# Where TensorE's operands begin in SBUF: one place mod 256 for high and low moving weights, and the row order of two-row pieces

## The chip, the cores and the metric

One NeuronCore of a Trainium2 chip runs the whole program in one launch. The metric is the device time in microseconds (us), the median of several executions. A profile of one execution stands beside it; its span runs from the first to the last instruction of the program.

## The reference: what is computed

Two transformer blocks on one sequence of 256 tokens of width 1024, all in float32. The first block normalises `x`, projects it with `w_in` into differential attention (8 heads), retention (4 heads) and two gates, mixes both branches, and adds a feed-forward layer (1024 to 4096 and back) and a gated embedding. The second block has an mLSTM mixer and a gated feed-forward layer with a causal convolution of width 3:

```python
def conv_ffn(x, w_up, conv_w, conv_b, w_down):
    u = causal_dwconv(x @ w_up, conv_w, conv_b)
    gate = u[..., :D_FF_2]
    val = u[..., D_FF_2:]
    return (jax.nn.silu(gate) * val) @ w_down      # 2816 rows in, 1024 columns out
```

A last RMS norm gives the output, 256 x 1024.

## The kernel before, in words

**Products in three passes.** Each operand of a large product is split into a high part (the value rounded to the matmul's `float32r` format, by ScalarE, line 198) and a low part (the rest, by VectorE, line 208). A product is then high x high + low x high + high x low, three matmuls (called passes, `q` = 0, 1, 2) that add up in PSUM. The low x low term is left out.

**Slabs.** All weights come in slabs of 1024 rows by 256 columns, in a fixed order (`_plan`). A slab has two halves of four 128-row pieces, and each half is one load of 512 KB, one high tile `hi_<slab>_<half>` and one low tile `lo_<slab>_<half>`. Loads go through a ring of four `raw` buffers on the SyncE queue; high and low tiles have rings of six. The down projection's slabs `dn0` to `dn10` are 256 rows by 1024 columns instead.

**Steps.** Three kinds of steps use the slabs, and they differ in which operand is stationary (loaded into the array by LDWEIGHTS) and which is moving (streamed through it):
- `b` steps (`pe_b`, line 257): the weights are stationary, activations move. Most slabs: `q`, `k`, `ga`, `gb`, `wd`, `wr`, `wo`, `f1`, `f2` (both named `f` in profiles), `pg`, `mq`, `mk`, `mw`, `ug`, `uv`, and likewise `wp` (lines 967 to 969).
- `a` steps (`pe_a`, line 267, and `step_wide`, line 340, for `mv0` alone): the activations are stationary and the weights move. Slabs `va0` to `va3`, `vr0` to `vr3`, `gr0` to `gr3`, `mv0` to `mv3`, `mo0` to `mo3`.
- the down projection (`pe_down`, line 1389): activations `gh`, `gl` (high and low) are stationary, the weights `dn` move. 528 matmuls, with the pass that comes first rotating from one output piece to the next.

Every such matmul is 128x128 by 128x256. A slab of an `a` or `b` step has 48: two halves, two column (or token) halves, four rows, three passes. Within a half `_steps` sets the order: it cuts the rows into pieces and goes through each piece pass by pass. At hooks between steps stand transposes and small products of the attention, the retention and the mLSTM, many of them in plain float32 with two passes of the engine.

**Places.** A tile of the high or low ring is 1088 columns of four bytes, 17 x 256 bytes, and a big activation tile 2112 columns, 33 x 256 bytes. In the built program both rings begin at multiples of 256 bytes. So an operand begins at a multiple of 256 bytes plus its *place*: `slot_of` shifts a weight tile by 16 columns (64 bytes) per unit of place, and `_place` gives the unit for high and low by the slab's name. Activations have no shift, so they are at 0.

**Joint steps.** Seven pairs of slabs (`JOINT`, among them `pg0`+`pg1`, `mw0`+`mw1`, `ug0`+`uv0`) are taken together: rows 0 to 3 of both, then rows 4 and 5 of both, then 6 and 7 of both (`joint`). These last are the two-row pieces. A norm's product with two passes (`pv_n`) stands among them in `pg` and `ug`.

What else counts below: `tu_m` are the transposes of the mLSTM's output `hn`, which VectorE writes at line 801; `w_m` and `ws_m` are the mLSTM's decay weights.

Of the kernel before, what the change touches and what calls it, by code (L numbers as in the profile page):

```python
# [10 lines left out]
F32 = mybir.dt.float32  # L11
F32R = mybir.dt.float32r
# [4 lines left out]
P = 128  # L17
# [88 lines left out]
def _place(name):  # L106

    n = name[0:2]
    if n in ("gr", "mv") or name in ("dn4", "dn5", "dn6"):
        return 3, 3  # L110
    if n in ("va", "vr", "mo", "dn"):
        return 1, 3
    if n == "wp":
        return 0, 2
    return 3, 1


def _steps(ks, m):

    ks = list(ks)  # L120
    cuts = {(4, 0): (1, 3), (4, 1): (2, 2), (2, 0): (2,), (2, 1): (1, 1), (3, 0): (1, 2), (3, 1): (3,)}[len(ks), m]
    steps = []
    for n in cuts:
        steps += [(q, k) for q in range(3) for k in ks[:n]]
        ks = ks[n:]
    return steps
# [3 lines left out]
def block_kernel(ctx: ExitStack, tc: tile.TileContext, I, out):  # L130
# [5 lines left out]
    big = ctx.enter_context(tc.tile_pool(name="big", bufs=11))  # L136
    work = ctx.enter_context(tc.tile_pool(name="work", bufs=2))
    psum = ctx.enter_context(tc.tile_pool(name="psum", bufs=4, space=bass.MemoryType.PSUM))

    def bigt(name, dt=F32, cols=2048):  # L140
        return big.tile([P, 2112], dt, tag="big", name=name)[:, 0:cols]

    def c8(t):
        return t.rearrange("p (c t) -> p c t", t=T)
# [13 lines left out]
    def pr(ap):  # L158
        return ap.rearrange("p (c t) -> p c t", c=2)
# [23 lines left out]
    def slot_of(tag, i, s):  # L183

        name = slabs[i][0]
        kk, cw = len(_rows(slabs[i])[s]), _width(slabs[i])
        pitch = -(-cw // 64) * 64
        sh = 16 * _place(name)[tag == "lo"]
        t = wpool.tile([P, 1088], F32R, tag=tag, name=f"{tag}_{name}_{s}", bufs=NBUF)
        return t[:, sh:sh + kk * pitch].rearrange("p (k n) -> p k n", k=kk)[:, :, 0:cw]  # L190
# [58 lines left out]
    def pe_b(ps, i, xh, xl, ks, m, start, stop):  # L249

        kk = geometry(i)[0]
        o = ps[:, m * T:(m + 1) * T]
        sl = slice(m * P, (m + 1) * P)
        steps = _steps(ks, m)
        for n, (q, k) in enumerate(steps):
            wv = (lo_t if q == 2 else hi_t)[i, k // kk]
            TE.matmul(o, lhsT=wv[:, k % kk, sl], rhs=(xl if q == 1 else xh)[:, k, :], start=start and n == 0,  # L257
                      stop=stop and n == len(steps) - 1, skip_group_check=True)

    def pe_a(ps, i, xh, xl, ks, t, start, stop):  # L260

        o = ps[:, t * T:(t + 1) * T]
        ts = slice(t * P, (t + 1) * P)
        steps = _steps(ks, t)
        for n, (q, k) in enumerate(steps):
            wv = (lo_t if q == 2 else hi_t)[i, k // 4]
            TE.matmul(o, lhsT=(xl if q == 1 else xh)[:, k, ts], rhs=wv[:, k % 4, :], start=start and n == 0,  # L267
                      stop=stop and n == len(steps) - 1, skip_group_check=True)
# [60 lines left out]
    def step_wide(name, xh, xl):  # L329

        i = index[name]
        cw = _width(slabs[i])
        pss = [mmbank(f"ps_{name}_0"), aux(f"ps_{name}_1")]

        def piece(s):
            for t in range(2):
                ts = slice(t * P, (t + 1) * P)
                ks = _rows(slabs[i])[s]
                for q, k in _steps(ks, t):
                    TE.matmul(pss[t][:, 0:cw], lhsT=(xl if q == 1 else xh)[:, k, ts],  # L340
                              rhs=(lo_t if q == 2 else hi_t)[i, s][:, k - ks[0], :], start=k == 0 and q == 0,
                              stop=k == 7 and q == 2, skip_group_check=True)

        halves(i, piece)
        after(i)
        return pss
# [42 lines left out]
    with tc.manual_schedule():  # L389
        S.preload_act_table_set(LNEXP)  # L390

        x = bigt("x0")
        xT = c8(x)
        par = const.tile([P, NPAR + PAD], F32, name="par")[:, 0:NPAR]
# [18 lines left out]
        nc.gpsimd.dma_start(out=ident, in_=I["c_ident"])  # L413
        lamt = wk("lamt", 768, tag="lg")[:, 0:T].rearrange("p (j d) -> p j d", j=4)
        cD = bigt("cD")
        maskT = const.tile([P, 384], F32, name="maskT")

# [10 lines left out]
        def rs_act(v, w, name, parts=P):  # L428
# [3 lines left out]
            return y0  # L432

        hh, hl = bigt("hh", F32R), bigt("hl", F32R)
        hhv, hlv = c8(hh), c8(hl)
        goff = _offsets()
# [32 lines left out]
        def split_plain(src, hv, lv):  # L469
            S.activation(hv, src, ACTF.Copy)  # L470
            yield
            V.tensor_tensor(out=lv, in0=src, in1=hv.bitcast(F32), op=ALU.subtract)
# [127 lines left out]
        va = bigt("va").rearrange("p (t n) -> p t n", t=2)  # L600
# [191 lines left out]
        gr, ga = bigt("gr").rearrange("p (t n) -> p t n", t=2), c8(bigt("ga"))  # L792
# [494 lines left out]
        gh, gl = {}, {}  # L1287
# [18 lines left out]
        def conv(ps, c0, s, name):  # L1306
            y = pr(ring[:, s % 4, :])
            u = pr(ps)
            if s < 2 * NRAWUP:
                u = pr(wk(f"u_{name}", 512, tag="qt"))  # L1310
                V.tensor_tensor(out=u, in0=pr(ps), in1=b2(r6), op=ALU.mult)
                yield
            for c in range(2):
                cc = c0 + c
                S.activation(y[:, c, :], u[:, c, :], ACTF.Identity, scale=cvt[:, 88 + cc:89 + cc], bias=cvt[:, 132 + cc:133 + cc])
            yield
            for c in range(2):
                cc = c0 + c
                V.scalar_tensor_tensor(out=y[:, c, 1:T], in0=u[:, c, 0:T - 1], scalar=cvt[:, 44 + cc:45 + cc], in1=y[:, c, 1:T],
                                       op0=ALU.mult, op1=ALU.add)  # L1320
                V.scalar_tensor_tensor(out=y[:, c, 2:T], in0=u[:, c, 0:T - 2], scalar=cvt[:, cc:cc + 1], in1=y[:, c, 2:T],
                                       op0=ALU.mult, op1=ALU.add)
            yield
# [10 lines left out]
        def post_uv(j):  # L1334
            def f(ps):
                yield from conv(ps, 22 + 2 * j, 2 * j + 1, f"v{j}")
                y = pr(ring[:, (2 * j + 1) % 4, :])
                V.tensor_tensor(out=y, in0=ug.pop(j), in1=y, op=ALU.mult)
                yield
                b, r = divmod(2 * j, 8)  # L1340
                if r == 0:
                    gh[b], gl[b] = c8(bigt(f"gh{b}", F32R)), c8(bigt(f"gl{b}", F32R))
                yield from split_plain(y, gh[b][:, r:r + 2, :], gl[b][:, r:r + 2, :])
            return f

# [30 lines left out]
        cuts = {0: ((0, 512), (512, 1024)), 1: ((0, 512), (512, 768), (768, 1024))}  # L1376
# [175 lines left out]
```

## Time and profile before

| what | value |
|---|---|
| median of three executions | 777.93 us (777.71 to 779.04) |
| the profiled execution | 778.0 us, span 776.2 us |
| TensorE busy | 765.4 us, 99% of the span |
| VectorE / ScalarE busy | 568.4 us, 73% / 464.6 us, 60% |
| DMA | 141.77 MB, mean 183 GB/s |

Matmuls are pipelined, so a matmul's own duration (276 to 287 ns) says little about how many go through. What counts is the distance between two starts. In a timeline, merged rows have a start, a time and a count: the start of the next row less the start of this one, over this row's count, is the pace. In the chain of work that ended last, a piece's time over its count gives the same for a longer run.

### The profile page before, as it was taken

What the parts mean: (1) busy time and instruction counts of PE and PEld (TensorE: products, weight loads), DVE (VectorE), ACT (ScalarE), POOL (GpSimd) and SP (SyncE); (2) the same over time, 40 slices, a digit from 0 to 9 for tenths busy, and PEclk for the clock granted to TensorE, in tenths of its full rate; (3) what the DMA queues carried; (4) which work ended last, traced back from release to release, by engine and by line L of the source; (5) the groups of instructions that cost most, each with busy time, mean ns of one, the idle gap of its engine ahead of it and who ended that gap; (6) DMA issues with size and microseconds to landing.
All of it is one profiled execution on the core that took longest, in us unless ns stands there. A gap on an engine that the chain in (4) does not pass through costs nothing.

```text
span 776.2 us, 16098 instructions
## 1 busy us (share of the span) xinstructions
PE 765.4 (99%) x6592; PEld 758.9 (98%) x6592; DVE 568.4 (73%) x895; ACT 464.6 (60%) x788; POOL 2.2 (0%) x8
## 2 busy tenths in 40 slices
PE   8999999999999999999999999999999999999996
PEld 8999999999999999999999999998999999999996
DVE  6887889566767678667555568897978988997433
ACT  6665656765754447656444457666866666766332
POOL 0000000000000000000000000000000000000000
PEclk9999999999999999999999999999999999999999
DMA  7775453555666556666666654364455556776621
GB/s 281 263 252 175 151 162 128 161 164 164 193 205 190 181 187 213 192 193 199 203 196 195 193 179 132 129 226 155 134 193 164 168 179 223 227 225 181 205 87 54
DMA packets 40473, 141.77 MB, mean 183 GB/s; under 512 B 4640, under 2 KB 5024, under 8 KB 40400
## 3 DMA queue, kind: packets, MB, share of 16 engines
q1 hardware_dynamic: 40032, 140.02, 57.2%
q8 instruction: 51, 0.84, 0.4%
q0 software_dynamic: 224, 0.72, 0.3%
q14 instruction: 22, 0.18, 0.1%
q10 hardware_dynamic: 144, 0.00, 0.0%
HBM read 139.68 MB, written 1.05 MB: 181 GB/s over the span
## 4 chain that ended last, share of the span: by engine, by line
PE 92%; DVE 3%; ACT 2%; DMA 1%; issue 1%; SPq 0%; ACTq 0%; DVEq 0%
PE ps_f L257 22%; PE acc L1389 8%; PE ps_ug L257 8%; PE ps_uv L257 8%; PE ps_vr L267 3%; PE ps_va L267 3%; PE ps_mo L267 3%; PE ps_mw L257 3%; PE ps_gb L257 3%; PE ps_gr L267 3%; PE ps_ga L257 3%; PE ps_wo L257 3%; PE ps_wr L257 3%; PE ps_wd L257 3%; PE ps_q L257 3%; PE ps_k L257 3%
## 5 line engine op out<-in xcount | busy, mean ns | idle before, releaser
L208 DVE TENSOR_TENSOR lo_f<-raw_f,hi_f 128x1024 fp32r<-128x1024 f32 x64 | 77.7, 1224 | 46.9 <-ACT hi_f L198 46.9
L198 ACT ACTIVATE hi_f<-raw_f 128x1024 fp32r<-128x1024 f32 x64 | 67.6, 1061 | 72.2 <-PE ps_f L257 64.1
L257 PE MATMUL ps_f<-h2h,hi_f 128*128 128x256 f32 x256 | 50.7, 277 | 0.0
L257 PE MATMUL ps_f<-h2l,hi_f 128*128 128x256 f32 x256 | 50.5, 276 | 0.0
L257 PE MATMUL ps_f<-h2h,lo_f 128*128 128x256 f32 x256 | 50.5, 276 | 0.0
L257 PE MATMUL ps_f<-ah,hi_f 128*128 128x256 f32 x256 | 49.9, 276 | 0.0
L257 PE MATMUL ps_f<-ah,lo_f 128*128 128x256 f32 x256 | 49.8, 276 | 0.0
L257 PE MATMUL ps_f<-al,hi_f 128*128 128x256 f32 x256 | 49.8, 276 | 0.0
L208 DVE TENSOR_TENSOR lo_dn<-raw_dn,hi_dn 128x1024 fp32r<-128x1024 f32 x22 | 26.9, 1224 | 22.7 <-ACT hi_dn L198 22.7
L198 ACT ACTIVATE hi_dn<-raw_dn 128x1024 fp32r<-128x1024 f32 x22 | 23.3, 1061 | 30.8 <-PE acc L1389 25.1
L1389 PE MATMUL acc<-hi_dn,gl 128*128 128x256 f32 x176 | 41.4, 280 | 0.0
L1389 PE MATMUL acc<-lo_dn,gh 128*128 128x256 f32 x176 | 41.3, 280 | 0.0
L1389 PE MATMUL acc<-hi_dn,gh 128*128 128x256 f32 x176 | 39.2, 280 | 0.0
L257 PEld LDWEIGHTS ps_f<-h2h,hi_f 128*128 128x128 f32 x256 | 38.9, 188 | 0.0
L257 PEld LDWEIGHTS ps_f<-h2l,hi_f 128*128 128x128 f32 x256 | 38.8, 188 | 0.0
L257 PEld LDWEIGHTS ps_f<-h2h,lo_f 128*128 128x128 f32 x256 | 38.8, 188 | 0.0
L257 PEld LDWEIGHTS ps_f<-ah,hi_f 128*128 128x128 f32 x256 | 38.6, 188 | 0.0
L257 PEld LDWEIGHTS ps_f<-ah,lo_f 128*128 128x128 f32 x256 | 38.5, 188 | 0.0
L257 PEld LDWEIGHTS ps_f<-al,hi_f 128*128 128x128 f32 x256 | 38.5, 188 | 0.0
L1389 PEld LDWEIGHTS acc<-lo_dn,gh 128*128 128x128 f32 x176 | 31.5, 188 | 0.0
L1389 PEld LDWEIGHTS acc<-hi_dn,gl 128*128 128x128 f32 x176 | 31.4, 188 | 0.0
L208 DVE TENSOR_TENSOR lo_ug<-raw_ug,hi_ug 128x1024 fp32r<-128x1024 f32 x22 | 26.5, 1220 | 5.5 <-ACT hi_ug L198 5.5
(482 smaller groups left out, 2519.9 us busy)
## 6 DMA issues: line engine op xcount, KB each, us to landing
raw_f<-in_w_dram SPq DMA_DIRECT2D x64, 512.0 KB, 3.8
raw_ug<-in_w_dram SPq DMA_DIRECT2D x22, 512.0 KB, 4.2
raw_uv<-in_w_dram SPq DMA_DIRECT2D x22, 512.0 KB, 4.3
raw_dn<-in_w_dram SPq DMA_DIRECT2D x22, 512.0 KB, 4.3
raw_va<-in_w_dram SPq DMA_DIRECT2D x8, 512.0 KB, 4.3
raw_vr<-in_w_dram SPq DMA_DIRECT2D x8, 512.0 KB, 3.6
raw_gr<-in_w_dram SPq DMA_DIRECT2D x8, 512.0 KB, 3.5
raw_ga<-in_w_dram SPq DMA_DIRECT2D x8, 512.0 KB, 4.0
```

The source lines that it names most:

```text
L198: S.activation(hi_t[i, s], raw_t[i, s], ACTF.Copy)
L208: V.tensor_tensor(out=lo_t[i, s], in0=raw, in1=hi_t[i, s].bitcast(F32), op=ALU.subtract)
L257: TE.matmul(o, lhsT=wv[:, k % kk, sl], rhs=(xl if q == 1 else xh)[:, k, :], start=start and n == 0, stop=stop and n == len(steps) - 1, ski ...
L267: TE.matmul(o, lhsT=(xl if q == 1 else xh)[:, k, ts], rhs=wv[:, k % 4, :], start=start and n == 0, stop=stop and n == len(steps) - 1, skip ...
L1389: TE.matmul(o, lhsT=(gl if q == 1 else gh)[b][:, r, ts], rhs=(lo_t if q == 2 else hi_t)[i, s][:, 0, f:f + T], start=k == 0 and n == 0 and ...
```

## The change

It does three things. (1) `_place`: the high and low weights of a slab that moves (`va`, `vr`, `gr`, `mv`, `mo`, `dn`) now begin at one place: 1 for `dn` and for seven named slabs, 3 for the others. Before, `va`, `vr`, `mo` and most `dn` slabs had the high part at 1 and the low part at 3, and `gr`, `mv`, `dn4` to `dn6` both at 3. (2) The low activations `gl` of the down projection begin 2 x 64 = 128 bytes further than the high ones. The tile already has 64 columns to spare. (3) `_steps`: in the second column half a two-row piece goes as one cut (pass by pass over both rows) and no longer row by row.

```diff
 def _place(name):
     n = name[0:2]
-    if n in ("gr", "mv") or name in ("dn4", "dn5", "dn6"):
+    if n == "dn" or name in ("va0", "va1", "vr2", "vr3", "gr1", "mv1", "mv2"):
+        return 1, 1
+    if n in ("va", "vr", "gr", "mv", "mo"):
         return 3, 3
-    if n in ("va", "vr", "mo", "dn"):
-        return 1, 3
     if n == "wp":
         return 0, 2
     return 3, 1
...
-    cuts = {(4, 0): (1, 3), (4, 1): (2, 2), (2, 0): (2,), (2, 1): (1, 1), (3, 0): (1, 2), (3, 1): (3,)}[len(ks), m]
+    cuts = {(4, 0): (1, 3), (4, 1): (2, 2), (2, 0): (2,), (2, 1): (2,), (3, 0): (1, 2), (3, 1): (3,)}[len(ks), m]
...
-    def bigt(name, dt=F32, cols=2048):
-        return big.tile([P, 2112], dt, tag="big", name=name)[:, 0:cols]
+    def bigt(name, dt=F32, cols=2048, place=0):
+
+        return big.tile([P, 2112], dt, tag="big", name=name)[:, 16 * place:16 * place + cols]
...
-                    gh[b], gl[b] = c8(bigt(f"gh{b}", F32R)), c8(bigt(f"gl{b}", F32R))
+                    gh[b], gl[b] = c8(bigt(f"gh{b}", F32R)), c8(bigt(f"gl{b}", F32R, place=2))
```

Only (3) moves instructions, and on TensorE alone. The two places that matter below are the last rows of the joint steps. TensorE, rows 4 and 5 of `pg0` (`h3h` and `h3l` are the high and low activations, `hi_pg`, `lo_pg` the weights), as they stand before the two-pass product (rows 6 and 7, behind it, read alike); before:

```order
L257 MATMUL ps_pg_5834<-h3h,hi_pg_1_5746 128x256 x2
L257 MATMUL ps_pg_5834<-h3l,hi_pg_1_5746 128x256 x2
L257 MATMUL ps_pg_5834<-h3h,lo_pg_1_5748 128x256 x2
L257 MATMUL ps_pg_5834<-h3h,hi_pg_1_5746 128x256
L257 MATMUL ps_pg_5834<-h3l,hi_pg_1_5746 128x256
L257 MATMUL ps_pg_5834<-h3h,lo_pg_1_5748 128x256
L257 MATMUL ps_pg_5834<-h3h,hi_pg_1_5746 128x256
L257 MATMUL ps_pg_5834<-h3l,hi_pg_1_5746 128x256
L257 MATMUL ps_pg_5834<-h3h,lo_pg_1_5748 128x256
```

and in the changed kernel (its lines are one higher):

```order
L258 MATMUL ps_pg_5834<-h3h,hi_pg_1_5746 128x256 x2
L258 MATMUL ps_pg_5834<-h3l,hi_pg_1_5746 128x256 x2
L258 MATMUL ps_pg_5834<-h3h,lo_pg_1_5748 128x256 x2
L258 MATMUL ps_pg_5834<-h3h,hi_pg_1_5746 128x256 x2
L258 MATMUL ps_pg_5834<-h3l,hi_pg_1_5746 128x256 x2
L258 MATMUL ps_pg_5834<-h3h,lo_pg_1_5748 128x256 x2
```

The second column half changed between high and low weights twice and now does so once. The same holds in `mw`, TensorE, rows 4 and 5 of `mw1`; before:

```order
L257 MATMUL ps_mw_7252<-hsh,hi_mw_1_7190 128x256 x2
L257 MATMUL ps_mw_7252<-hsl,hi_mw_1_7190 128x256 x2
L257 MATMUL ps_mw_7252<-hsh,lo_mw_1_7200 128x256 x2
L257 MATMUL ps_mw_7252<-hsh,hi_mw_1_7190 128x256
L257 MATMUL ps_mw_7252<-hsl,hi_mw_1_7190 128x256
L257 MATMUL ps_mw_7252<-hsh,lo_mw_1_7200 128x256
L257 MATMUL ps_mw_7252<-hsh,hi_mw_1_7190 128x256
L257 MATMUL ps_mw_7252<-hsl,hi_mw_1_7190 128x256
L257 MATMUL ps_mw_7252<-hsh,lo_mw_1_7200 128x256
```

and now:

```order
L258 MATMUL ps_mw_7252<-hsh,hi_mw_1_7190 128x256 x2
L258 MATMUL ps_mw_7252<-hsl,hi_mw_1_7190 128x256 x2
L258 MATMUL ps_mw_7252<-hsh,lo_mw_1_7200 128x256 x2
L258 MATMUL ps_mw_7252<-hsh,hi_mw_1_7190 128x256 x2
L258 MATMUL ps_mw_7252<-hsl,hi_mw_1_7190 128x256 x2
L258 MATMUL ps_mw_7252<-hsh,lo_mw_1_7200 128x256 x2
```

The number of matmuls is the same; the rows of VectorE, ScalarE, GpSimd and SyncE stand as before.

## Rows read from the trace of the kernel before

**Rows 1.** The page: TensorE's busy time, share of the span and count (with the other engines'), and the shares of the chain that ended last by engine.

```profile
PE 765.4 (99%) x6592; PEld 758.9 (98%) x6592; DVE 568.4 (73%) x895; ACT 464.6 (60%) x788; POOL 2.2 (0%) x8
...
PE 92%; DVE 3%; ACT 2%; DMA 1%; issue 1%; SPq 0%; ACTq 0%; DVEq 0%
```

**Rows 2.** Who waited for whom, TensorE alone: us in total, times, longest.

```profile
PE my L577 <- DVE w_m L566: 1.3, 1, 1.3
PE ps_q L257 <- ACT hi_q L488: 1.1, 3, 0.4
PE warm L411 <- DVE epst L408: 1.1, 1, 1.1
PE my L578 <- DVE ws_m L570: 0.2, 1, 0.2
```

**Rows 3.** Busy time by stretch: the stretch, its length, then busy us (and count) of PE, PEld, DVE, ACT, POOL, the granted clock, the DMA engines' share, GB/s. The stretches are `va`, `mo`, and the end of `ug`/`uv` with the first half of `dn`.

```profile
18.00:43.00 25.00, 25.00 (x211) 24.52 (x210) 22.37 (x38) 16.60 (x29) 0.00 (x0) 1.00 0.79 269
543.00:562.00 19.00, 19.00 (x165) 19.00 (x164) 17.69 (x49) 16.69 (x43) 0.00 (x0) 1.00 0.39 122
684.00:745.00 61.00, 61.00 (x529) 61.00 (x528) 40.84 (x54) 32.27 (x39) 0.00 (x0) 1.00 0.66 198
```

**Rows 4.** The chain of work that ended last, in order of time, its longest runs: start us, us, what and how many.

```profile
291.23 160.52 PE ps_f L257 x1416
543.87 14.14 PE ps_mo L267 x120
...
707.02 62.08 PE acc L1389 x528
```

**Rows 5.** The same chain: two slabs of `va`, then the four slabs of `gr`.

```profile
31.29 11.50 PE ps_va L267 x96
...
138.03 5.46 PE ps_gr L267 x48
...
144.81 5.66 PE ps_gr L267 x48
...
152.41 5.46 PE ps_gr L267 x48
...
159.82 5.46 PE ps_gr L267 x48
```

**Rows 6.** The timeline of TensorE in `gr2`: start us, us, engine, line, operation, out<-in, count.

```profile
152.61 0.50 PE L267 MATMUL ps_gr<-hi_gr,hh 128*128 128x256 f32 x3
152.95 0.50 PE L267 MATMUL ps_gr<-hi_gr,hl 128*128 128x256 f32 x3
153.29 0.50 PE L267 MATMUL ps_gr<-lo_gr,hh 128*128 128x256 f32 x3
```

**Rows 7.** The same in `gr1`.

```profile
145.00 0.52 PE L267 MATMUL ps_gr<-hi_gr,hh 128*128 128x256 f32 x3
145.35 0.52 PE L267 MATMUL ps_gr<-hi_gr,hl 128*128 128x256 f32 x3
145.70 0.52 PE L267 MATMUL ps_gr<-lo_gr,hh 128*128 128x256 f32 x3
146.06 0.40 PE L267 MATMUL ps_gr<-hi_gr,hh 128*128 128x256 f32 x2
```

**Rows 8.** The same in `ug4`, from the second column half of its first half to the start of its second.

```profile
631.94 0.40 PE L257 MATMUL ps_ug<-h7l,hi_ug 128*128 128x256 f32 x2
632.18 0.39 PE L257 MATMUL ps_ug<-h7h,lo_ug 128*128 128x256 f32 x2
632.41 0.28 PE L257 MATMUL ps_ug<-h7h,hi_ug 128*128 128x256 f32 x1
632.52 0.28 PE L257 MATMUL ps_ug<-h7l,hi_ug 128*128 128x256 f32 x1
632.63 0.28 PE L257 MATMUL ps_ug<-h7h,lo_ug 128*128 128x256 f32 x1
```

**Rows 9.** The same in `wp`: its first three matmuls and its twelfth.

```profile
451.58 0.28 PE L967 MATMUL ps_wp<-pTh,hi_wp 128*128 128x256 f32 x1
451.70 0.28 PE L968 MATMUL ps_wp<-pTl,hi_wp 128*128 128x256 f32 x1
451.81 0.28 PE L969 MATMUL ps_wp<-pTh,lo_wp 128*128 128x256 f32 x1
...
452.83 0.28 PE L969 MATMUL ps_wp<-pTh,lo_wp 128*128 128x256 f32 x1
```

**Rows 10.** The same at the start of the down projection (`dn0`).

```profile
706.86 0.28 PE L1389 MATMUL acc<-hi_dn,gh 128*128 128x256 f32 x1
706.97 0.28 PE L1389 MATMUL acc<-hi_dn,gl 128*128 128x256 f32 x1
707.08 0.28 PE L1389 MATMUL acc<-lo_dn,gh 128*128 128x256 f32 x1
707.20 0.28 PE L1389 MATMUL acc<-hi_dn,gl 128*128 128x256 f32 x1
```

**Rows 11.** The same in `mv1` (510.56) and in the second half of `mv2` (519.58).

```profile
510.56 0.52 PE L267 MATMUL ps_mv<-hi_mv,h4h 128*128 128x256 f32 x3
510.91 0.52 PE L267 MATMUL ps_mv<-hi_mv,h4l 128*128 128x256 f32 x3
...
519.58 0.50 PE L267 MATMUL ps_mv<-hi_mv,h4h 128*128 128x256 f32 x3
519.92 0.50 PE L267 MATMUL ps_mv<-hi_mv,h4l 128*128 128x256 f32 x3
```

**Rows 12.** The chain of work in order of time, from 476 to 535 us, its longest piece (a load).

```profile
506.45 5.45 DMA raw_mv<-in_w_dram
```

**Rows 13.** The timelines of VectorE (`hn` for the first transposes `tu_m`) and of TensorE (those transposes).

```profile
555.51 1.67 DVE L801 SCALAR_TENSOR_TENSOR hn<-hn,mc,og 128x256 f32<-128x256 f32 x4
...
557.85 0.82 PE L808 MATMUL tu_m<-ident,hn 128*128 128x128 f32 x6
```

**Rows 14.** The chain of work: the joint step `pg0`+`pg1` with `pg2`, `pg3`, before and after its two-pass product, and `mw` before and after its last transposes.

```profile
457.19 8.17 PE ps_pg L257 x72
...
465.79 10.82 PE ps_pg L257 x94
...
562.16 5.55 PE ps_mw L257 x48
...
568.15 16.58 PE ps_mw L257 x144
```

## The prediction, made before the run

> **What bounds the kernel now.** First the page: TensorE is busy for 765.4 of 776.2 us, and its work makes 92% of the chain that ended last [rows 1]. The table of waits shows hardly any idle time on it: 3.7 us in six waits, 1.5 of them for the mLSTM weights `w_m` and `ws_m` [rows 2]. [...]
>
> Then the chain in order of time, which groups long runs of matmuls. 1416 matmuls of the `f` stage take 160.52 us, 113.4 ns each. The down projection takes 62.08 us for 528, 117.6 ns each, and the output gate `mo` 14.14 us for 120, 117.8 ns [rows 4]. All are 128x128 by 128x256; only the operands' places differ. The retention gate slabs `gr` are the instructive ones, since they are equal in everything that the code sets: `gr0`, `gr2` and `gr3` take 5.46 us for 48 (113.75 ns) and `gr1` takes 5.66 (117.9) [rows 5]. The timeline shows how. After its first matmuls `gr2` makes every group of three in 0.34 us; `gr1` makes every group of three in 0.35 to 0.36, to its end [rows 6, 7]. So there are **two paces**, about 113.4 and 117.8 ns, and a slab with one place for high and low weights keeps the pace it falls into.
>
> What can move it from one to the other? In the `b` steps (weights stationary at places 3 and 1, that is 128 bytes apart) the pace of 113 survives every change between high and low: 1416 matmuls without a break [rows 4]. And a slow start gets out: in `ug4` the groups of two come every 0.23 to 0.24 us up to 632.18, the next starts are 0.23, 0.11 and 0.11 apart [rows 8]. In the `a` steps with **moving** weights at places 1 and 3, `va`, 96 matmuls take 11.50 us, with no such stretch [rows 5]. I read this as two SBUF reads, of the moving operand and of the next weights, that disturb each other in a way that depends on where they stand to each other. A shift of the stationary operand by 128 bytes leaves a good relation good; a shift of the moving operand by 128 bytes breaks it. The relation itself is my inference; the rows show the paces.
>
> **The change part by part.**
>
> *Down projection, 528 matmuls.* Now the moving weights are at place 1 (dn0 to dn3, dn7 to dn10, high part; low part 3) or at 3. Afterwards all are at 1, and of the stationary activations `gl` lies 128 bytes further than `gh`. That is moving 64, stationary 0 or 128, changing from one matmul to the next. One stage of the old kernel has exactly this: `wp`, with moving activations at 64 (as the built program places them) and stationary weights at 0 (high) or 128 (low). It comes after a `b` step, as dn0 does, and its starts are 0.12, 0.11 and on average 0.114 us apart (1.25 us for the eleven distances to its twelfth matmul) [rows 9]. The entry into dn0 today agrees: its first two matmuls, still at place 1, are 0.11 us apart, and 0.12 appears with the low weights at place 3 [rows 10]. So 117.58 falls to 113.36 ns: 528 x 4.22 = 2.23 us, less 0.05 for the entry, **2.18 us**. Bounds: 2.23, and -0.1 if all of it stays at 117.8 (528 x 0.2). I take the upper end, since `wp` is the nearest row. This stage's feeders have room: in the stretch around its start VectorE is busy for 40.84 of 61 us and ScalarE for 32.27 [rows 3].
>
> *The `a` steps, 13 slabs* (va0 to va3, vr0 to vr3, gr1, mo0 to mo3): each 48 matmuls, 117.8 now and 113.75 if it falls into the better pace, 48 x 4.05 = 0.19 us a slab, 2.53 us for all. Each slab gets one place, and so keeps the pace in which it starts. Which one is the open point. At place 3 the starts seen are three of four in `gr`, `mv2`'s second half at 0.34 per three, and `mv1` at 0.35 to 0.36 [rows 5, 11]: four good of six. At place 1 the only rows are the entries of `wp` and dn0, both good [rows 9, 10]. The table keeps place 3 for `gr0`, `gr2`, `gr3` and `mv3`, and gives place 1 to `gr1`, `mv1` and `mv2`. By four in six 8.7 of 13 slabs would gain, 1.69 us; by the place 1 rows all. I take 10, **1.95 us**; bounds 0 (all start badly; 117.8 is what they cost now) and 2.53.
>
> *`mv1`, `mv2`.* Up to 72 matmuls could win 0.3 us, but I price them at **0**: from 476 to 535 us the chain runs mostly over ScalarE, VectorE and a load (`raw_mv`, 5.45 us), and PE then waits 1.3 us for `w_m` [rows 2, 12]. An earlier PE waits longer there.
>
> *`mo`* is interrupted by the transposes `tu_m` at 557.85, whose `hn` VectorE ends at 555.51 + 1.67 = 557.18 [rows 13]. VectorE is busy for 17.69 of 19 us there [rows 3]. 168 matmuls before it give 0.68 us, the slack is 0.67, so I take back **0.1 us** (bounds 0 and 0.4, if VectorE stays where it is and the rest of the gain too is late).
>
> *Two-row pieces.* Only the joint steps have them. A second column half with (1,1) went high, high, low for one row and then for the next; with (2,) it goes like the first half. `pg` takes 8.17 us for 72 before its two-pass product and 10.82 for 94 after it: 113.5 against 115.1 ns; over 113.4 that is 94 x 1.7 = 0.16 us. `mw` has 192 matmuls, 5.55 + 16.58 = 22.13 us, 0.36 over 113.4 [rows 14]. `ug` has the same break as `pg`. `ug4` got out of the slow pace in groups of two, two, two [rows 8], which is the new order; in `pg` 24 matmuls with the old one did not. Together 0.16 + 0.36 + 0.16; I take somewhat less than half, **0.25 us** (bounds -0.1, since a new order may also lose a good relation, and 0.68). Instruction counts, DMAs, and the orders of ScalarE, VectorE, GpSimd and SyncE do not move, so no queue is passed; the tiles' sizes do not change either.
>
> *Cover.* `va` is where gains could be eaten: VectorE is busy for 22.37 of 25 us [rows 3], and 0.8 us less would make it 92%. The table of waits names nothing of `va` [rows 2], so I take 0 back; the price, if it is too late, is at most those 0.6 to 0.8 us.
>
> *Sum.* 2.18 + 1.95 + 0 - 0.1 + 0.25 = 4.28 us. The profiled execution took 778.0 us (span 776.2 and 1.8 around it), 0.07 over the median of 777.93. 778.0 - 4.3 = **773.7 us**.
>
> **The rivals.**
>
> *A, only a third of the `a` slabs get the better pace.* For: `gr1` and `mv1`, one place and slow throughout. Four of 13 give 0.8: gain 2.18 + 0.8 + 0.15 = 3.1, 774.9 us.
>
> *B, the down projection stays slow.* For: dn4 to dn6 have one place already, and the stage as a whole runs at 117.6 [rows 4]; `wp` changes places in a fixed rhythm of three while the down projection rotates. Against: the entry. Gain 1.95 + 0.15 = 2.1, 775.9 us.
>
> *C, places have nothing to do with it.* The two paces would come from what the other engines read and write at the time; `gr1` and `gr2` have equal places and different paces, which speaks for it. 1416 even matmuls beside busy ScalarE and VectorE speak against it. Then only the joint order acts: 778.0, within 0.3. [...]
>
> *D, slower: place 1 is a bad place for a moving operand.* Its place is the down projection. If every change between `gh` and `gl` costs a late start as the worst ones there do today (0.12 us and over where the weights change [rows 10]; say 122 ns), two matmuls in three are such: 352 x (122 - 117.6) = 1.5 us more, and the slabs with place 1 gain nothing either. With no gain at place 3: 779.5 us. It decides from a mean of 121 ns on, where it eats the 1.95 us of the `a` slabs (528 x 3.7). Against it stands `wp`, whose moving operand lies at 64 [rows 9].
>
> **How the numbers follow.** The forecast has a chance of 0.55, A 0.22, B 0.11, C 0.08, D 0.04. The range of 8 in 10 reaches from all parts at their upper end but `mv` (2.23 + 2.53 + 0.68 = 5.4 us, 772.6, and 0.2 for the spread of the runs, 772.4) to B and a little over it, 776.3; C and D are left out, and some of B. A measurement of this kernel tells 0.2%, 1.6 us, from no change. Faster by more: forecast, A, and most of B, 0.87. Within: C, the rest of B and a little of D, 0.10. Slower: the rest of D, 0.03.
>
> **What would show it.** In the chain, `acc` x528 at 59.9 us instead of 62.08 and the `va` run of 96 at 10.9 to 11.1 instead of 11.50; in the timeline of every `a` slab groups of three in 0.34 us from the second group on, or 0.35 to its end (A). Wrong would be: `acc` still over 61.5 us (B or C), a wait for `w_m` that is longer by more than 0.4 us (a gain lost in the mLSTM), or a new wait of `tu_m` for `hn` or of `va` for its low weights.

## The result, and the profile after

The changed kernel takes **774.0 us** (median of four executions, 773.48 to 774.69), the kernel before in the same comparison 778.01 us (four, 777.71 to 779.04). The ratio is 0.9947, with an interval of 0.9929 to 0.9964: 4.0 us less, where 4.3 were forecast. The profiled execution took 774.69 us with a span of 772.3, 3.9 less than before.

From the page, the busy time of the engines, which answers to [rows 1]:

```profile
PE 760.3 (98%) x6592; PEld 753.9 (98%) x6592; DVE 568.0 (74%) x895; ACT 464.4 (60%) x788; POOL 2.2 (0%) x8
```

TensorE is busy for 5.1 us less, the other engines for as long as before. Two rows of the table of waits, TensorE alone (us in total, times, longest), beside [rows 2]; the other two read as before:

```profile
PE ps_q L258 <- ACT hi_q L489: 2.1, 3, 1.0
PE my L578 <- DVE w_m L567: 1.3, 1, 1.3
```

No wait is new; `w_m` is waited for as long as before. The one that grew stands in the first 18 us, ahead of any changed slab (more on it below). The chain in order of time (start us, us, what and how many), beside [rows 4, 5, 14]:

```profile
31.81 11.09 PE ps_va L268 x96
...
108.87 5.46 PE ps_vr L268 x48
...
115.52 5.65 PE ps_vr L268 x48
...
122.91 5.85 PE ps_vr L268 x48
...
144.47 5.66 PE ps_gr L268 x48
...
290.84 160.52 PE ps_f L258 x1416
...
465.41 10.75 PE ps_pg L258 x94
...
535.56 5.46 PE ps_mo L268 x48
543.17 13.62 PE ps_mo L268 x120
...
557.67 2.74 PE ps_mo L268 x24
...
566.83 16.33 PE ps_mw L258 x144
...
705.37 59.85 PE acc L1390 x528
```

The same view of the kernel before, with what was not shown ahead of the prediction:

```profile
108.83 5.65 PE ps_vr L267 x48
...
115.66 5.86 PE ps_vr L267 x48
...
536.08 5.66 PE ps_mo L267 x48
...
558.88 2.84 PE ps_mo L267 x24
```

The gain by stage, before less after: down projection 62.08 - 59.85 = 2.23 us; `mo` 0.20 + 0.52 + 0.10 = 0.82; `va` 11.50 - 11.09 = 0.41, of `va2` and `va3` alone; `vr` 0.19 + 0.21 = 0.40, of `vr0` and `vr1` alone; `gr` 0; `pg` 0.07 and `mw` 0.25 behind their two-pass products and transposes; `ug` 0.09, of which 0.04 in its joint step (11.43 us before, 11.39 now) and 0.05 in the slab `ug1` behind it (5.49 and 5.44). The starts of the runs tell where it arrived. The `va` run begins 0.52 us later than before, `f` 0.39 earlier, the long run of `mo` 0.70, the down projection 1.65, and it ends 3.88 us earlier.

The timeline of TensorE (start us, us, engine, line, operation, count) shows the better pace in `va2`, now at place 3:

```profile
32.19 0.50 PE L268 MATMUL ps_va<-hi_va,hh 128*128 128x256 f32 x3
32.53 0.50 PE L268 MATMUL ps_va<-hi_va,hl 128*128 128x256 f32 x3
```

That is 0.34 us for a group of three, and so on to the slab's end. `gr1`, now at place 1, still takes 0.35 to 0.36 for three, much as in [rows 7].

### The profile page after: what moved, and what is told of

The parts are those of the page before. It is cut to its first block, busy times and chain, and to the rows that moved or that the text cites. A ratio compares the mean times of both kernels' runs of the same rounds, so it can differ in the third digit from the quotient of the medians.

```text
span 772.3 us, 16098 instructions
## 1 busy us (share of the span) xinstructions
PE 760.3 (98%) x6592; PEld 753.9 (98%) x6592; DVE 568.0 (74%) x895; ACT 464.4 (60%) x788; POOL 2.2 (0%) x8
## 4 chain that ended last, share of the span: by engine, by line
PE 91%; DVE 3%; DMA 2%; ACT 2%; issue 1%; SPq 0%; ACTq 0%; DVEq 0%
PE ps_f L258 23%; PE ps_ug L258 8%; PE ps_uv L258 8%; PE acc L1390 8%; PE ps_vr L268 3%; PE ps_va L268 3%; PE ps_gr L268 3%; PE ps_gb L258 3%; PE ps_mw L258 3%; PE ps_mo L268 3%; PE ps_ga L258 3%; PE ps_wo L258 3%; PE ps_wr L258 3%; PE ps_wd L258 3%; PE ps_q L258 3%; PE ps_k L258 3%
```

## Experiments

The runs of each comparison were timed against the kernel before on the same chip; the ratio with its interval is to that kernel. The first two take the down projection by itself.

**One place for `dn` and the shift of `gl`, alone (e1).** Edit of the kernel before:

```diff
+    if n == "dn":
+        return 1, 1
-    if n in ("gr", "mv") or name in ("dn4", "dn5", "dn6"):
+    if n in ("gr", "mv"):
         return 3, 3
-    if n in ("va", "vr", "mo", "dn"):
+    if n in ("va", "vr", "mo"):
         return 1, 3
...
-                    gh[b], gl[b] = c8(bigt(f"gh{b}", F32R)), c8(bigt(f"gl{b}", F32R))
+                    gh[b], gl[b] = c8(bigt(f"gh{b}", F32R)), c8(bigt(f"gl{b}", F32R, place=2))
```

> The kernel before with only the down projection's part: its weights at place 1, high and low, and the low activations 128 bytes further. Theory (the places set the pace): the run of 528 in the chain at 59.9 us as in the changed kernel, 2.2 us less than before, 775.8 us; all stages ahead of it as before. Rival (the pace comes from what the other engines do, and only the earlier arrival changed it): the run of 528 stays at 62.08, 778.0 us.

**The same without the shift of `gl` (e2).** The last pair of lines is left as it was.

> As the one before, but the low activations begin at the same place as the high ones, so that neither operand ever shifts by 128 bytes. Theory (a shift of the stationary operand lets a slow stream escape; without one a stream keeps the pace in which it starts or into which a disturbance throws it): it enters at 113.4 ns behind the gated layer's steps and falls to 117.8 at some disturbance, without return; the run of 528 between 59.9 and 62.2 us, most likely 61, 777 us. Rival (one place for the weights is all that counts, the shift of the activations does nothing): 59.9 us and 775.8 us, the same as with the shift.

Measured: 775.73 us (0.9966, 0.9954 to 0.9979) and 776.57 us (0.9978, 0.9968 to 0.9988). The chain of e1, two of its runs:

```profile
31.16 11.50 PE ps_va L269 x96
...
706.60 59.85 PE acc L1391 x528
```

and of e2:

```profile
32.22 11.50 PE ps_va L269 x96
...
707.73 59.85 PE acc L1391 x528
```

The down projection takes 59.85 us in both. So one place for the weights is what acts, and the shift of `gl` adds nothing to it: the theory lost against its rival in e2. The two totals don't contradict this. Their intervals overlap, the profiled execution of e2 (776.47 us) stands near its median, and it was already 1.06 us late at `va`, though up to there both programs issue the same instructions at the same places. By that much these two executions differed in the first 30 us, and the 0.52 us by which the changed kernel was late there is less.

**Broken in `dn0`, with and without the shift (e5, e6).** Edit of the changed kernel; e6 has `place=0` for `gl` besides:

```diff
     if n == "dn" or name in ("va0", "va1", "vr2", "vr3", "gr1", "mv1", "mv2"):
-        return 1, 1
+        return 1, (3 if name == "dn0" else 1)
```

> The changed kernel, but dn0's low weights at place 3 again, so that 48 matmuls of the down projection are thrown into the slow pace; from dn1 on all weights stand at place 1 and the low activations 128 bytes further. Theory (a shift of the stationary operand by 128 bytes lets a slow stream escape): dn0 at 117.5 ns, 0.2 us more, and the better pace again soon after dn1 begins; the run of 528 at 60.1 us, 774.2 us. Rival (the shift of the activations does nothing, as the kernel without it suggests): slow to the end, 62.0 us, 776.1 us.

> As the one before, but the low activations begin where the high ones do: from dn1 on nothing shifts. Theory (with constant places a stream keeps the pace it has): slow to the end, 62.0 us for the run of 528, 776.1 us, as dn4 to dn6 of the kernel before were slow behind dn3. Rival (place 1 by itself is the better place and brings a stream back): 60.1 us, 774.2 us.

**Other distances between the operands (e7, e11).** Edits of the changed kernel: in e7 `return 2, 2` for `dn`; in e11 `place=1` for `gl`, 64 bytes.

> The changed kernel with the down projection's weights at place 2 in place of 1, so that moving and stationary operands lie 0 or 128 bytes apart mod 256 and no longer 64 or 192. Theory (the two reads disturb each other by their relative place, and every stream seen at 113.4 ns had 64 or 192 between them): slower than 117.8 ns or as slow, the run of 528 at 62.0 us or more, 776.1 us or more. Rival (only a change of the moving operand's place counts): 59.85 us, 774.0 us.

> The changed kernel with the low activations of the down projection 64 bytes further instead of 128, so that moving and stationary operands lie 64 bytes apart with gh and 0 with gl. Theory (the relative place decides: 64 and 192 good, 0 and 128 bad): a third of the matmuls, those with gl, are at a bad place, the run of 528 between 60.5 and 62.7 us, most likely 61.5, 775.7 us. Rival (only the moving operand's place must stay): 59.85 us, 774.0 us.

Measured: e5 774.33 us (0.9952, 0.9937 to 0.9967), e6 776.43 (0.9977, 0.9968 to 0.9986), e7 776.59 (0.9978, 0.9968 to 0.9987), e11 775.3 (0.9962, 0.9948 to 0.9976). The down projection in the chains of e5, e6, e7 and e11:

```profile
705.14 60.15 PE acc L1389 x528
```

```profile
704.99 62.18 PE acc L1389 x528
```

```profile
704.72 62.72 PE acc L1391 x528
```

```profile
704.37 61.75 PE acc L1389 x528
```

All four went as the theory said. The stream that was thrown into the slow pace got out where the stationary operand shifted by 128 bytes (e5, 60.15 us, 0.30 lost) and stayed in it to the end where nothing shifted (e6, 62.18 us, 117.8 ns each). With 0 or 128 bytes between moving and stationary operand the run took 118.8 ns each on average (e7), with 64 and 0 in turn 117.0 (e11).

Taken alone, e7 could mean that place 2 is a bad place for a moving operand, and e11 that a shift of 64 bytes disturbs where one of 128 does not. The end of e11 decides between these and the distance. The last 96 matmuls do four of one pass and then four of the next, with all weights at place 1. TensorE there:

```profile
755.78 0.62 PE L1389 MATMUL acc<-lo_dn,gh 128*128 128x256 f32 x4
756.23 0.62 PE L1389 MATMUL acc<-hi_dn,gh 128*128 128x256 f32 x4
756.69 0.64 PE L1389 MATMUL acc<-hi_dn,gl 128*128 128x256 f32 x4
757.17 0.62 PE L1389 MATMUL acc<-lo_dn,gh 128*128 128x256 f32 x4
```

Four with `gh`, 64 bytes apart, take 0.45 to 0.46 us, four with `gl`, 0 apart, take 0.48. Inside the groups of four, where no operand's place changes, the starts are 113.3 ns apart with `gh` and 119.8 with `gl`, over all 96. So here the distance of 0 was slow by itself, and the next group with `gh` was at the better pace again. When e5 gets out is seen in TensorE's timeline, at the start of `dn1`'s second half:

```profile
713.55 0.28 PE L1389 MATMUL acc<-hi_dn,gl 128*128 128x256 f32 x1
713.67 0.28 PE L1389 MATMUL acc<-lo_dn,gh 128*128 128x256 f32 x1
713.78 0.28 PE L1389 MATMUL acc<-hi_dn,gl 128*128 128x256 f32 x1
```

The first two are 0.12 us apart, the next 0.11, and so it goes on: 72 matmuls were slow, 24 of them in `dn1`. These runs also decide rival C (the other engines' traffic sets the pace). From 710 to 764 us, all in the down projection, the busy time by engine (length, then PE, PEld, DVE, ACT, POOL, granted clock, DMA share, GB/s) of e5 and e6:

```profile
710.00:764.00 54.00, 54.00 (x478) 54.00 (x477) 25.35 (x30) 19.61 (x25) 0.00 (x0) 1.00 0.40 120
```

```profile
710.00:764.00 54.00, 54.00 (x461) 54.00 (x460) 24.26 (x27) 18.29 (x22) 0.00 (x0) 1.00 0.39 119
```

The neighbours do as much, rather more in e5, the clock is 1.00 in both, and e5 gets 17 matmuls more through. The two differ in the place of `gl` alone.

**A shift of the first block's low activations (e8).** Edit of the changed kernel:

```diff
-        hh, hl = bigt("hh", F32R), bigt("hl", F32R)
+        hh, hl = bigt("hh", F32R), bigt("hl", F32R, place=2)
```

> The changed kernel with the low activations hl of the first block 128 bytes further. They are stationary in va, vr and gr (12 slabs) and moving in q, k, qr, kr, ga and gb (20 slabs). Theory (a shift of the stationary operand lets a slow stream escape, one of the moving operand breaks a good one): va0, va1, vr2, vr3 and gr1 get into the better pace in their first groups, 1.0 us less; the 20 slabs fall to 117.8 ns, up to 4.2 us more; 777 us in all. Rival (shifts of activations do nothing either way): 774.0 us, with the same slabs slow as in the changed kernel.

Measured: 776.62 us (0.9982, 0.9972 to 0.9991), 2.6 more than the changed kernel. From its chain: `va1`'s second half, `va2` with `va3`, then `vr2`, `vr3`, a slab of `gb`, and `f`:

```profile
27.82 2.75 PE ps_va L267 x24
...
31.42 11.10 PE ps_va L267 x96
...
124.19 5.86 PE ps_vr L267 x48
131.03 5.47 PE ps_vr L267 x48
...
190.19 5.66 PE ps_gb L257 x48
...
293.48 160.52 PE ps_f L257 x1416
```

From the `va` run of 96 to `f` it takes 262.06 us, the changed kernel 259.03. The part on moving operands held: every `q`, `k`, `gb` slab in its chain is at 5.65 us or more for 48 (5.45 to 5.69 in the changed kernel), and 3.0 us net are lost where 3.2 were expected. The part on stationary operands held only in part. `vr3` (5.47 us) and `va1`'s second half (2.75, in the changed kernel 2.83) get out; `vr2` (5.86), `gr1` (5.67) and the two halves between those of `va0` and `va1` (5.67 for 48) don't. `va0`'s first half is good here too (2.75 us for 24), but it is so in some runs without the shift (see below). So the shift let a stream out in two of five places, and in e5 only after 24 matmuls of `dn1`.

**The other cut of the two-row pieces, alone (e4).** Edit of the kernel before: `(2, 1): (2,)` for `(2, 1): (1, 1)` in `_steps`.

> The kernel before with only the other cut of the two-row pieces in the second column half. Theory: in pg, mw, ug0+uv0 the slow stretch ends inside the joint step, 0.4 us less there, and the first joint step (q0, k0) starts 0.5 us later as in the changed kernel, so 778.0 us and no difference. Rival (the late start of the first joint step in the changed kernel has another cause): 0.4 us less, 777.6 us, with k0 ending as early as before.

Measured: 777.69 us against 778.38 (0.9991, 0.9982 to 1.0): 0.7 us less by the medians, but the interval reaches no change. The chain of e4, `pg` and `mw` behind their interruptions:

```profile
465.86 10.74 PE ps_pg L257 x94
...
567.54 16.38 PE ps_mw L257 x144
```

0.08 us less in `pg`, 0.20 in `mw`, 0.09 in `ug` as in the changed kernel, and no late start (the `va` run of 96 begins at 31.35 against 31.29): the rival's side, the cut is not what made the changed kernel late.

**Why five slabs stay slow: places (e3), a further matmul (e9, e10), what runs ahead (e12).** In the changed kernel `va0`, `va1`, `vr2`, `vr3` and `gr1` kept 117.8 ns. e3 gives them, and `mv2`, place 3 (only `dn` and `mv1` keep 1). e9 and e10 put one more matmul ahead of the last three, of 64 and of 256 columns:

```diff
         def piece(s):
+            if s == 0 and name in ("vr2", "vr3", "gr1"):
+                TE.matmul(ps[:, 0:64], lhsT=xh[:, 0, 0:P], rhs=hi_t[i, 0][:, 0, 0:64], start=True, stop=True)
```

e12 has `gr1` at place 3 and in the retention `enumerate((18, 19, 21, 22))` for `enumerate((18, 20, 21, 22))`, the hooks at which the heads are computed.

> The changed kernel with place 3 in place of 1 for va0, va1, vr2, vr3, gr1 and mv2 (mv1 stays at 1). Theory (behind a two-pass float32 product a stream at place 1 starts in the slow pace, one at place 3 mostly in the better one): four or five of the five slabs of va, vr and gr fall to 113.8 ns, 0.2 us each, mv2's second half gains 0.1 us: 0.8 to 1.1 us less, 773.0 us. Rival (where a slab stands in the program decides, not its place): these slabs stay at 117.8, 774.0 us.

> The changed kernel with one more matmul, of 64 columns, ahead of the first of vr2, vr3 and gr1 (its result is overwritten); places as they are. Theory (a stream at constant places keeps the pace into which its start throws it, and what the engine did just before decides that): the other start changes the pace of at least one of the three slabs from 117.8 to about 113.6 ns, 0.2 us each, for 0.05 us a matmul; 773.6 to 774.0 us. Rival (these slabs are slow for a reason that lasts, such as what the other engines read and write beside them): all three stay at 117.8 ns, 774.2 us.

> As the one before with 256 columns in place of 64, so that the further matmul is like those of the slab. Theory: it only makes the slab one matmul longer, so the start stays as it was and the three slabs stay at 117.8 ns: 774.35 us (3 x 0.118 more). Rival (any further matmul between the two-pass products and the slab brings the better pace): three times 0.2 less 0.12, 773.75 us.

> The changed kernel with gr1 at place 3, and the scores of the second retention head (rs<-qkr, two-pass float32 products) one slab earlier, ahead of gr0 instead of gr1; its product ry with the values, in float32r, moves with it and stands right ahead of gr1. Nothing else in gr1 changes. Theory (what the engine ran just ahead of a slab decides its pace): gr1 starts as gr0 did, behind ry, and takes 5.46 us for 48 instead of 5.66; gr0 starts behind rs as gr2 and gr3 do and keeps its 5.46; 0.2 us less, 773.8 us. Rival (gr1 is slow for a reason of its own, since neither place 3 nor place 1 nor a further matmul ahead of it helped): 5.66 again, 774.0 us.

Measured: e3 773.75 us (0.9944, 0.9931 to 0.9956), e9 774.2 (0.9946, 0.9931 to 0.9961), e10 774.05 (0.9947, 0.9932 to 0.9962), e12 774.43 (0.9951, 0.9935 to 0.9968); none can be told from the changed kernel's 774.0. In e3 the five slabs stayed slow, at 117.8 ns or more, against the theory. Two of them in its chain, `vr2` and `gr1`:

```profile
123.33 5.86 PE ps_vr L267 x48
...
144.90 5.66 PE ps_gr L267 x48
```

In e9 and e10 the three stayed slow (5.73 to 5.74 us for 48 in the chain of e9, 5.65 to 5.66 in that of e10), in e9 too, where the theory expected at least one to change. TensorE in `vr2` of e9, 0.36 us for three:

```profile
123.53 0.51 PE L267 MATMUL ps_vr<-hi_vr,hl 128*128 128x256 f32 x3
123.89 0.52 PE L267 MATMUL ps_vr<-lo_vr,hh 128*128 128x256 f32 x3
```

In the chain of e12, `gr0` and `gr1`:

```profile
139.15 5.66 PE ps_gr L267 x48
...
146.55 5.46 PE ps_gr L267 x48
```

Here `gr1` is at the better pace for the first time; against e3, nothing is changed in it but what runs ahead, and with that the other engines' work for this head, which moved too. And `gr0`, behind `rs` here, is now at the slow one. In all 13 other traces it is the other way round, `gr0` good (5.46 us) and `gr1` slow (5.66 to 5.74). The first half of the expectation holds, the second not: 0.2 us won and lost. So the pace was no property of the slab or of its one place: at place 3 `gr1` took 5.66 us in e3 and 5.46 here, and what differed is what stood around its start. But "behind `rs`" does not sort the slabs. Ahead of `rs` stood a wait at `gr0` of e12 (slow), `py` at `gr1` of the changed kernel (slow) and transposes `pyt` at `gr2` of e12 (good):

```profile
138.22 0.70 PE L714 MATMUL rs<-qkr 128*128 128x256 f32 x2 [0.51 <-ACT ysq L676]
...
143.43 0.39 PE L666 MATMUL py<-va,aT 128*128 128x128 f32 x2
...
151.85 0.38 PE L690 MATMUL pyt<-ident,ya 128*128 128x128 f32 x2
```

`gr2` and `gr3` of the changed kernel are good with `ry` ahead of `rs`, and its `vr3` is slow with other transposes (`pa`) there. Behind the scores `sc` it is no clearer: `va2` and `vr1` of the changed kernel are good (0.34 us for three), `vr2` is slow (0.35 to 0.36), and so it is at place 3 (e3, 5.86 us for 48).

**One late start, seen in `va0`.** The changed kernel and e5, e6, e7, e9, e10, e11 and e12 have the same instructions at the same places in `va0`, and in all eight it follows `k0` directly, with its first starts 0.113 to 0.117 us apart. In five (e5, e6, e7, e10, e12) its first half stays at 113.3 ns. In three (the changed kernel, e9, e11) the fourth matmul starts 0.15 to 0.17 us after the third, and from there the half goes at 117.8. TensorE in the changed kernel, then in e10, from the third matmul on:

```profile
19.03 0.31 PE L268 MATMUL ps_va<-lo_va,hh 128*128 128x256 f32 x1
19.18 0.51 PE L268 MATMUL ps_va<-hi_va,hh 128*128 128x256 f32 x3
19.54 0.51 PE L268 MATMUL ps_va<-hi_va,hl 128*128 128x256 f32 x3
```

```profile
19.35 0.28 PE L267 MATMUL ps_va<-lo_va,hh 128*128 128x256 f32 x1
19.47 0.50 PE L267 MATMUL ps_va<-hi_va,hh 128*128 128x256 f32 x3
```

In e10 the next group follows at 19.81, 0.34 us later; in the changed kernel at 0.36. So in these three one start that was 0.04 to 0.06 us late went with the slow pace for the rest of the half. In the five good ones `va0`'s second half is slow, behind a two-pass norm product (`pv_n`), at 5.65 to 5.66 us for the 48 matmuls of it and of `va1`'s first half: there the pace changed at an interruption inside a slab. Why the fourth matmul was late in some executions, and what makes one interruption throw a stream and another not, stays open.

## Why the prediction was right, by its steps

**The bound.** TensorE's pace was the price: TensorE is busy for 5.1 us less, and no listed wait behind the first 18 us moved. The granted clock was 1.00 in `va`, `mo` and around the start of the down projection, as before [rows 3].

**Down projection.** 2.18 us forecast, 2.23 measured, 113.35 ns each as in `wp` [rows 9]. But half of the reason was wrong. I took the shift of `gl` for a part of it; e2 shows that a constant place of the weights, 64 bytes from `gh` and `gl`, was enough behind a `b` step that was already at the better pace (59.85 us). The shift helped only the stream that was thrown out before (60.15 us in e5 against 62.18 in e6). The inference from the paces, two reads that disturb each other by their relative place, was only argued then. e7 and e11 now show the part on relative places: with the same instructions, 59.85, 61.75 and 62.72 us follow from the operands' places, and e6 against e2 shows that behind `dn0` one set of places went at 117.8 or at 113.4 ns. That it is two reads that collide, and how, is not shown.

**The `a` steps.** The step that was mis-sized: 10 of 13 slabs forecast, 1.95 us; 8 came, 0.82 + 0.41 + 0.40 = 1.63 us. The five others are those with place 1, and I had counted on the place 1 rows [rows 9, 10], whose entries were undisturbed. A count of places could not size this term: at 3 the five are as slow (e3), `gr1` is good with other neighbours (e12), and `va0` was good or slow by one late start. That a stream at one place keeps its pace was right in the changed kernel for every stretch without interruption in `va`, `vr`, `gr` and `mo` (groups of three at 0.34 us, or at 0.35 to 0.36, to its end), but for the three matmuls ahead of that late start. And it is a stretch that keeps it and not a slab: `mv2` and, in five runs, `va0` changed between their halves. Nothing of the gain was eaten in `va`, where VectorE had been the worry.

**`mv1`, `mv2`** were priced at 0. `mv1` does run in the better pace now (0.34 us for three), and so does `mv2`'s first half. `mv2`'s second half, at place 1, lost it: its groups of three start at 518.78 and 519.14, 0.36 apart, where they took 0.34 before [rows 11]. From `f`, 0.39 us early, to the long run of `mo`, 0.70 early, `pg` gave 0.07 and `mo0` 0.20; what is left for `mv` is 0.04. The reason was nearly the one given. The last group of `mv3` starts 0.69 us earlier than before (529.14 against 529.83), but the first product `my` behind it only 0.52 (529.64 against 530.16): its `ws_m` comes from ScalarE at 529.59, against 530.12. So 0.17 us was lost ahead of `ws_m`; the wait for `w_m` stayed at 1.3 us.

**`mo`.** 0.1 us was to be lost to `hn`. The table of waits has no row of `tu_m`, and 0.82 us arrived whole.

**Two-row pieces.** 0.25 us forecast, 0.07 + 0.25 + 0.09 = 0.41 measured in `pg`, `mw` and `ug`. The cut alone gives 0.08 + 0.20 + 0.09 (e4), so nearly all of it is the cut. I had taken less than half of what was to be had, and more than half came. In `pg` the slow stretch ended inside the joint step, as read from `ug4` [rows 8]: in TensorE's timeline the six matmuls up to 467.37 us take 0.71 us, the next six 0.68.

**Sum.** 2.23 + 1.63 + 0.41 = 4.27 us by these rows, 0.52 lost at the start, as executions differ there. That leaves 3.75 of the 3.9 us by which the span shrank; the rest is 0.04 in `mv` and short pieces that I did not follow. That the parts add up to the 4.28 forecast is in part luck: the `a` steps gave 0.32 less, and the down projection, `mo` and the two-row pieces together 0.31 more.

**Rivals.** A (4 of 13 slabs) did not come; 8 did, nearer to the 10 of the forecast. B fell with the run of 528 and D with the same, since at place 1 it took 59.85 us. C fell with e5 against e6 (60.15 and 62.18 us) and with the end of e11. Its best argument, `gr1` and `gr2` with equal places and different paces, is answered by the two paces at one set of places, though what else ran beside a slab's start was not ruled out as what throws it.

## What to carry to other kernels

Where the timeline shows matmuls of one shape at two paces (here 113.4 and 117.8 ns), look at where their operands begin before looking at the other engines, and try first the places that were good here. The run of 528 took 62.08 us with the moving operand's place changing between passes in most slabs, and 59.85 with it kept, 64 bytes mod 256 from the stationary operand (e2) or 64 and 192 in turn (e1); with 0 and 128 it took 62.72 (e7). A shift of 128 bytes on the stationary side cost nothing in that run (e1 against e2); on the moving side it took `q`, `k` and `gb` to 5.65 us or more for 48 (e8), from 5.45 to 5.69. Constant places did not bring a slow stream back (e6, 62.18 us). Test each part of such a change by itself; here one part of three did nothing in the run of 528. An order without needless changes between high and low weights cost nothing here and won 0.4 us.

## What the runs showed of the hardware that was not expected

- The paces of the 128x128 by 128x256 float32r matmuls in the down projection went with where their operands begin: 113.4 ns with 64 bytes between them and constant places (e2), 117.8 with the same places behind a disturbance (e6), 118.8 on average with 0 and 128 in turn (e7), 119.8 with 0 in a row (the end of e11).
- Two paces lasted at one and the same set of places: in e6 the slow one for the 480 matmuls behind `dn0` (62.18 us for all 528), in e2 the good one for all 528 (59.85 us). In the first half of `va0` the three runs with one start that was 0.04 to 0.06 us late went on at 117.8 ns, the five without it at 113.3.
- One more matmul ahead of `vr2`, `vr3` and `gr1` left them slow (5.73 to 5.74 us for 48 with 64 columns in e9, 5.65 to 5.66 with 256 in e10); with another order of the products ahead of it `gr1` took 5.46 us and `gr0` 5.66 (e12), against 5.66 and 5.46 in the changed kernel.
- Two executions of the same instructions differed by 1.06 us at 32 us into the program (e1, e2).
